# One hold fewer in a scaled copy: the fifth tile loaded whole, the third tile's stores issued right behind that load

## The chip, the core and the metric

The kernel runs on one core of a Trainium2 chip. The core has a vector engine (DVE in the profile), a scalar engine (ACT), a GpSimd engine (POOL), a tensor engine that this kernel doesn't use, and a sync engine (SP) whose sequencer issues DMA transfers. Sixteen DMA engines carry the transfers between the chip's memory (HBM, named "dram" in the profile) and the on-chip memory (SBUF, 128 partitions). The metric is the device time of one execution in microseconds. The kernel before took 239.05 us, the median of three runs (238.97 to 239.15).

## The reference

Each of 16 x 1024 tokens is a row of 512 floats. Each token goes to two experts, and its row is written twice, each time scaled by that expert's weight:

```python
def reference(x, expert_indices, expert_weights):
    batch, seq, hidden = x.shape          # 16, 1024, 512, float32
    k = expert_indices.shape[-1]          # 2
    x_expanded = x[:, :, np.newaxis, :].repeat(k, axis=2)
    weights = expert_weights[..., np.newaxis]
    return (x_expanded * weights).astype(np.float32)
```

The indices' values are not used. The input x has 33.6 MB and the output 67.1 MB, so what is stored is twice what is loaded.

## The kernel before

The 16,384 tokens are 128 per partition. They are cut into five tiles along the tokens of a partition: `groups` = 25, 25, 25, 25 and 28 tokens per partition. A partition's tokens of one tile lie next to each other in the memory, so a transfer has one unbroken row per partition (25 tokens loaded are 51,200 bytes; a stored token is 4,096 bytes, since it is written twice).

Buffers: `x_pair` are two input buffers, used in turn by the tiles (tiles 0, 2, 4 use the first, 1 and 3 the second). `o_ring` is one output buffer of 25 tokens (`TX`), used by every tile, in two parts: tokens 0 to 12 and 13 to 24 (`CUT` = 13). `w_tile` has all weights.

Transfers: `move` issues a DMA from SP and keeps SP's issues in the order of the program. `load(i, e)` loads part e of tile i; `STEPS` says in which parts a tile comes (tile 0 as 9 and 16 tokens, tile 2 as 21 and 4, tile 4 as 24 and 4), and a tile that is not in `STEPS` comes whole. `store(dst, at, to)` writes tokens at to `to` of `o_ring` to the output. `wait(ins, done)` makes the transfer `ins` wait at its issue until the transfer `done` has landed. The framework adds the waits that the data need: a load waits until the tile that used its buffer before has been computed, a store until its half has been computed, and computing a half waits until the ring's half has been stored.

Work on a tile (the loop at the end of the kernel): for each of the two parts of the ring, DVE multiplies the first 8 tokens (9 in tile 0) by their weights in pieces of 4 tokens (`product`, line 97), and ACT the other 4 or 5 tokens, one row at a time (`scalar`, line 120). Then the transfers:

- Tiles 1, 3 and 4 issue each store as soon as its part is computed. Tile 1 also issues the load of tile 3 behind its stores.
- Tiles 0 and 2 are "held": first the load into the buffer that this tile has read (tile 2 or tile 4), in two parts, then the two stores, each made to wait until the first part of that load has landed. Tile 0 issues the weights of the other tiles between.
- Tile 4 has three tokens more than the ring; they are computed and stored at the end.

So SP issues in this order: loads 0, 1, 2 and the weights; stores of 0 (held) and 1; loads 3 and 4; stores of 2 (held), 3 and 4. All of them but the first weights go through one queue of SP (q1 in the profile), on line 66.

Of the kernel before, what the change touches and what calls it, by code (L numbers as in the profile page):

```python
# [1 line left out]

# [4 lines left out]


@with_exitstack
def kernel(  # L10
    ctx: ExitStack,
    tc: tile.TileContext,
    x: bass.AP,
    expert_indices: bass.AP,
    expert_weights: bass.AP,
    out: bass.AP,
):
    nc = tc.nc

    batch, seq, hidden = x.shape  # L20
    k = expert_weights.shape[-1]
    P = nc.NUM_PARTITIONS
    ntok = batch * seq
    assert ntok % P == 0
    A_TOTAL = ntok // P

    f32 = mybir.dt.float32
    row = k * hidden
    CH = 4


    groups = [25, 25, 25, 25, 28]
    TX = 25
    CUT = 13
    STEPS = {0: [9, 16], 2: [21, 4], 4: [24, 4]}
    assert sum(groups) == A_TOTAL

    xf = x.rearrange("b s h -> (b s) h")
    of = out.rearrange("b s k h -> (b s) (k h)")
    wf = expert_weights.rearrange("b s k -> (b s) k")  # L40

    w_pool = ctx.enter_context(tc.tile_pool(name="w_pool", bufs=1))
    x_pool = ctx.enter_context(tc.tile_pool(name="x_pool", bufs=1))
    o_pool = ctx.enter_context(tc.tile_pool(name="o_pool", bufs=1))

    w_tile = w_pool.tile([P, A_TOTAL * k], f32)
    o_ring = o_pool.tile([P, TX * row], f32)
    x_pair = [
        x_pool.tile([P, max(groups[e::2]) * hidden], f32, name=f"x{e}")
        for e in range(2)  # L50
    ]

    def rows(of_all, done, T):
        return of_all[done * P : (done + T) * P, :].rearrange(
            "(p a) n -> p (a n)", a=T
        )

    tiles = []
    done = 0
    for n in groups:  # L60
        tiles.append((done, n))
        done += n


    def move(out, in_):
        return tc.keep_in_program_order(nc.sync.dma_start(out=out, in_=in_))  # L66


    def wait(ins, done):
        tc.add_manual_dep(  # L70
            ins.ins,
            done.ins.name,
            mybir.DependencyInfo(
                mybir.DependencyClass.Sync, mybir.DependencyReason.DATA
            ),
            reason="turn",
        )

    def load(i, e):
        at = sum(STEPS.get(i, groups[i : i + 1])[:e])  # L80
        to = at + STEPS.get(i, groups[i : i + 1])[e]
        part = slice(at * hidden, to * hidden)
        return move(x_pair[i % 2][:, part], rows(xf, *tiles[i])[:, part])

    def weights(g, to):
        at, n = tiles[g]
        w = w_tile[:, at * k : (at + (to - g) * n) * k]
        return (
            w.rearrange("p (g m) -> p g m", g=to - g),
            wf[at * P : (at + (to - g) * n) * P, :].rearrange(  # L90
                "(g p a) n -> p g (a n)", g=to - g, p=P
            ),
        )

    def product(o_tile, t, x_in, c, m):
        o = t * row
        nc.vector.tensor_tensor(  # L97
            out=o_tile[:, o : o + m * row].rearrange(
                "p (t k h) -> p t k h", t=m, k=k
            ),  # L100
            in0=x_in[:, : m * hidden]
            .rearrange("p (t h) -> p t h", t=m)
            .unsqueeze(2)
            .to_broadcast([P, m, k, hidden]),
            in1=w_tile[:, c : c + m * k]
            .rearrange("p (t k) -> p t k", t=m)
            .unsqueeze(3)
            .to_broadcast([P, m, k, hidden]),
            op=mybir.AluOpType.mult,
        )  # L110


    def vector(src, c, at, to):
        for t in range(at, to, CH):
            u = min(t + CH, to)
            product(o_ring, t, src[:, t * hidden : u * hidden], c + t * k, u - t)

    def scalar(src, c, at, to):
        return [
            nc.scalar.mul(  # L120
                out=o_ring[:, e * hidden : (e + 1) * hidden],
                in_=src[:, e // k * hidden : (e // k + 1) * hidden],
                mul=w_tile[:, c + e : c + e + 1],
            )
            for e in range(at * k, to * k)
        ]

    def store(dst, at, to):
        return move(dst[:, at * row : to * row], o_ring[:, at * row : to * row])


    out_w, in_w = weights(0, 1)
    nc.scalar.dma_start(out=out_w, in_=in_w)
    load(0, 0)
    load(0, 1)
    load(1, 0)
    for i, (done, n) in enumerate(tiles):
        src, dst, c = x_pair[i % 2], rows(of, done, n), done * k
        v = 9 if i == 0 else 8
        held = i in (0, 2)  # L140
        for at, to in [(0, CUT), (CUT, TX)]:
            vector(src, c, at, at + v)
            scalar(src, c, at + v, to)
            if not held:
                store(dst, at, to)
        if held:
            if i == 0:
                last = load(2, 0)
                load(2, 1)
                for g in range(1, len(tiles)):  # L150
                    move(*weights(g, g + 1))
            else:
                last = load(4, 0)
                load(4, 1)
            for at, to in [(0, CUT), (CUT, TX)]:
                wait(store(dst, at, to), last)
        elif i == 1:
            load(3, 0)
        if n > TX:
            m = n - TX  # L160
            product(o_ring, 0, src[:, TX * hidden :], c + TX * k, m)
            move(dst[:, TX * row :], o_ring[:, : m * row])

# [1 line left out]
_INS = ['x', 'expert_indices', 'expert_weights']  # L165
_OUTS = [((16, 1024, 2, 512), 'float32')]


# [23 lines left out]
```

## Time and profile before

| | |
|---|---|
| median of 3 runs | 239.05 us |
| the profiled execution's own time | 238.92 us |
| its span, first to last instruction | 237.1 us |
| moved by DMA | 100.80 MB, 425 GB/s over the span |
| DVE busy | 93.1 us (39%) |
| ACT busy | 54.9 us (23%) |
| DMA queue q1 | 98.7% of the 16 engines' span |

The profile is of one execution. Times in it are counted from the start of its span. A line of the timeline or of the chain of waits begins with start and length in microseconds; a group line gives engine, line of the code, operation, what is written and read, and how many. An engine's name with a "q" behind it means its sequencer, which issues transfers and is not counted as busy. For a DMA issue, "us to landing" is the time from its issue to the end of the whole transfer, the time that it spends behind others in the queue included. The DMA share of a stretch is the time of the packets that start in it, over 16 engines and the stretch's length; for a stretch of the length of a few packets it can be far from the busy share, and above 1.

### The profile page before, as it was taken

The numbers are of one execution on the slowest core, as the hardware profiler recorded it, in microseconds if no ns is written. First come the engines' busy times: TensorE is split into PE (matmuls) and PEld (weight loads), VectorE is DVE, ScalarE is ACT, GpSimd is POOL, SyncE is SP. The second block draws the span as 40 slices with busy tenths as digits, with TensorE's granted clock in tenths as the row PEclk, the third lists the DMA queues.
The fourth block names the chain that finished last, engine by engine and source line by source line (L and its number), as shares of the span: only waits on it lengthen the run. The fifth ranks groups of instructions, "written<-read, shape, count | busy, mean of one in ns | idle before, by whom it ended". The sixth has DMA issues, their size and how long they took to land.

```text
span 237.1 us, 217 instructions
## 1 busy us (share of the span) xinstructions
DVE 93.1 (39%) x23; ACT 54.9 (23%) x87; POOL 0.2 (0%) x4
## 2 busy tenths in 40 slices
DVE  0499800000094580954900000039195292861300
ACT  0008800000090520914400000037080270800000
POOL 0000000000000000000000000000000000000000
DMA  7999989899999999999999999999999999999996
GB/s 260 474 445 475 423 370 464 372 486 431 420 398 497 464 431 420 398 398 409 475 478 406 398 453 431 431 409 457 484 431 431 409 398 434 449 449 456 423 398 265
DMA packets 3457, 100.80 MB, mean 425 GB/s; under 512 B 1024, under 2 KB 1024, under 8 KB 1024
## 3 DMA queue, kind: packets, MB, share of 16 engines
q1 hardware_dynamic: 3312, 100.77, 98.7%
q10 hardware_dynamic: 144, 0.03, 0.1%
q14 instruction: 1, 0.01, 0.0%
HBM read 33.69 MB, written 67.11 MB: 425 GB/s over the span
## 4 chain that ended last, share of the span: by engine, by line
DMA 70%; DVE 16%; ACT 4%; issue 3%; SPq 0%; DVEq 0%; ACTq 0%
DMA out_dram<-o_ring 46%; DMA x<-in_x_dram 24%; DVE o_ring L97 16%; ACT o_ring L120 3%; ACT L120 1%; SPq L66 0%; DVEq L97 0%; ACTq L120 0%
## 5 line engine op out<-in xcount | busy, mean ns | idle before, releaser
L97 DVE TENSOR_TENSOR o_ring<-x,w_tile 128x4096 f32<-128x4096 f32 (+2 forms) x23 | 93.1, 4096 | 128.5 <-DMA out_dram<-o_ring 105.6
L120 ACT ACTIVATE o_ring<-x,w_tile 128x512 f32<-128x512 f32 x86 | 53.7, 709 | 134.0 <-DMA out_dram<-o_ring 123.3
L120 ACT ACT_TABLE_LOAD x1 | 1.3, 1283 | 18.6 <-DMA x<-in_x_dram 18.6
L176 POOL MEMSET const-bfloat16-1.0<- 128x1 bf16 x1 | 0.1, 102 | 0.0
L176 POOL MEMSET const-uint8-127<- 128x1 uint8 x1 | 0.1, 102 | 0.0
L176 POOL MEMSET const-float32-0.0<- 128x1 f32 x1 | 0.1, 99 | 0.2 <-issue 0.2
L176 POOL MEMSET const-float32-1.0<- 128x1 f32 x1 | 0.1, 99 | 0.0
## 6 DMA issues: line engine op xcount, KB each, us to landing
out_dram<-o_ring SPq DMA_DIRECT2D x5, 6656.0 KB, 21.3
out_dram<-o_ring SPq DMA_DIRECT2D x5, 6144.0 KB, 21.6
x<-in_x_dram SPq DMA_DIRECT2D x2, 6400.0 KB, 34.1
x<-in_x_dram SPq DMA_DIRECT2D x1, 6144.0 KB, 20.6
x<-in_x_dram SPq DMA_DIRECT2D x1, 5376.0 KB, 18.8
x<-in_x_dram SPq DMA_DIRECT2D x1, 4096.0 KB, 17.4
x<-in_x_dram SPq DMA_DIRECT2D x1, 2304.0 KB, 8.1
x<-in_x_dram SPq DMA_DIRECT2D x2, 1024.0 KB, 21.4
```

What stands on the lines that cost most here:

```text
L97: nc.vector.tensor_tensor(out=o_tile[:, o : o + m * row].rearrange("p (t k h) -> p t k h", t=m, k=k), in0=x_in[:, : m * hidden] .rearrange ...
L120: nc.scalar.mul(out=o_ring[:, e * hidden : (e + 1) * hidden], in_=src[:, e // k * hidden : (e // k + 1) * hidden], mul=w_tile[:, c + e : c ...
L176: nc = _bacc.Bacc("TRN2", target_bir_lowering=False, num_devices=1)
```

## The change

Tile 4 leaves `STEPS`, so it is loaded in one piece of 28 tokens. Tile 2 is no longer held: its two stores are issued right behind the load of tile 4 and wait for nothing but their data. Tile 0 keeps its hold and its order. What the loop did for tiles 1, 3 and 4 stays as it was.

```diff
-    STEPS = {0: [9, 16], 2: [21, 4], 4: [24, 4]}
+    STEPS = {0: [9, 16], 2: [21, 4]}
...
-        held = i in (0, 2)
         for at, to in [(0, CUT), (CUT, TX)]:
             vector(src, c, at, at + v)
             scalar(src, c, at + v, to)
-            if not held:
+            if i in (1, 3, 4):
                 store(dst, at, to)
-        if held:
-            if i == 0:
-                last = load(2, 0)
-                load(2, 1)
-                for g in range(1, len(tiles)):
-                    move(*weights(g, g + 1))
-            else:
-                last = load(4, 0)
-                load(4, 1)
+        if i == 0:
+            last = load(2, 0)
+            load(2, 1)
+            for g in range(1, len(tiles)):
+                move(*weights(g, g + 1))
             for at, to in [(0, CUT), (CUT, TX)]:
                 wait(store(dst, at, to), last)
         elif i == 1:
             load(3, 0)
+        elif i == 2:
+            load(4, 0)
+            store(dst, 0, CUT)
+            store(dst, CUT, TX)
```

## The prediction

> **What bounds the kernel now.** I read the page first, then a table of stretches, then the chain of waits, then the queue's waits, and last single packets of the transfers around the edit.
>
> ```profile
> span 237.1 us, 217 instructions
> ...
> DVE 93.1 (39%) x23; ACT 54.9 (23%) x87; POOL 0.2 (0%) x4
> ...
> DMA  7999989899999999999999999999999999999996
> ...
> q1 hardware_dynamic: 3312, 100.77, 98.7%
> ```
>
> The two computing engines are idle most of the time; the 16 DMA engines are not. The table of stretches (length, busy time of the computing engines, clock, DMA share, GB/s) puts the edges to it:
>
> ```profile
> core 0: us, DVE busy (x) ACT busy (x) POOL busy (x), PEclk, DMA share, GB/s
> 0.00:1.74 1.74, 0.00 (x0) 0.00 (x0) 0.20 (x4) 1.00 0.00 0
> 1.74:235.90 234.16, 93.14 (x23) 54.95 (x87) 0.00 (x0) 1.00 1.00 430
> 235.90:237.10 1.20, 0.00 (x0) 0.00 (x0) 0.00 (x0) 1.00 0.00 0
> ```
>
> From the first packet at 1.74 to the last end at 235.90 the DMA share is 1.00. So the time is 1.74 of lead-in, 234.16 of packets without a gap worth 1%, and 1.20 of drain. Only three things can move it: fewer or shorter packets, a stretch in which the queue would have run dry, or a change in what a packet costs. Whether an engine waits longer or shorter for its data matters only if the queue runs dry through it.
>
> The chain of waits around the edit (start, length, what):
>
> ```profile
> 88.37 21.56 DMA out_dram<-o_ring
> ...
> 118.85 20.61 DMA x<-in_x_dram
> ...
> 139.52 18.14 DMA out_dram<-o_ring
> ...
> 157.85 8.77 DVE o_ring L97 x2
> ...
> 166.68 14.48 DMA out_dram<-o_ring
> ...
> 188.08 8.77 DVE o_ring L97 x2
> ```
>
> Here 88.37 is the second store of the second tile, 118.85 the first part of the fifth tile's load (24 tokens), 139.52 the third tile's first store, which was held until that load had landed (118.85 + 20.61 = 139.46), 157.85 the fourth tile's first half, which needs the ring that this store empties, and 188.08 the fifth tile's. The hold shows as one of SP's three waits for a load:
>
> ```profile
> SPq L66 <- DVE o_ring L97: 168.8, 10, 28.8
> SPq L66 <- DMA x<-in_x_dram: 41.9, 3, 19.8
> ```
>
> The longest, 19.8 us, is the hold that goes. But a wait of the queue's issuer is not a wait of the DMA engines, and the next steps keep the two apart.
>
> **The change part by part.**
>
> *The hold.* If it left the engines without work, the stretch around it would show it. In the same table, with windows cut to the packets (a packet counts with its whole time in the stretch in which it starts, so share times length is the mean packet time of an engine when each of the 16 starts one):
>
> ```profile
> 136.70:142.94 6.24, 0.00 (x0) 0.00 (x0) 0.00 (x0) 1.00 1.01 431
> 142.90:143.60 0.70, 0.00 (x0) 0.00 (x0) 0.00 (x0) 1.00 2.81 1217
> ```
>
> The first row runs from the last packets of the 24-token part, over the 4-token part, through the first packets of the held store. Share 1.01 times 6.24 is 6.30 us of packets in 6.24 us of time: the engines had work throughout. The 4-token part covers the hold (8 packets per engine of 0.31, below, 2.5 us, against about 1.0 from an issue to its first packet, estimated from the first load's issue at 0.73, in the timeline below, and its first packet at 1.74). So taking the hold away wins 0.00. Without that cover the hold would cost about 1 us; the change removes hold and cover together.
>
> *The load in one piece.* Three bands of 16 packets of different row lengths, 12 tokens stored (48 KB), 25 tokens loaded (50 KB), and above at 142.90 13 tokens stored (52 KB):
>
> ```profile
> 105.00:105.70 0.70, 0.00 (x0) 0.00 (x0) 0.00 (x0) 1.00 2.59 1123
> 106.80:107.50 0.70, 0.00 (x0) 0.00 (x0) 0.00 (x0) 1.00 2.75 1123
> 110.70:111.40 0.70, 0.70 (x1) 0.70 (x3) 0.00 (x0) 1.00 2.75 1170
> 112.60:113.30 0.70, 0.70 (x1) 0.70 (x2) 0.00 (x0) 1.00 2.70 1170
> ```
>
> 2.59, 2.70 and 2.81 times 0.70 are 1.813, 1.890 and 1.967 us: 0.077 for each 2 KB more, load or store alike. And inside the 4-token part, 62 packets of 8 KB in 1.2 us:
>
> ```profile
> DMA packets 62, 0.51 MB, mean 423 GB/s; under 512 B 0, under 2 KB 0, under 8 KB 0
> ...
> q1 hardware_dynamic: 62, 0.51, 100.2%
> ```
>
> 1.002 x 16 x 1.2 / 62 = 0.310 us. Each engine serves 8 rows of a tile. Before: 8 x (1.813 + 0.310) = 16.98. After: 8 rows of 56 KB, two steps above 52 KB, 8 x (1.967 + 0.154) = 16.97; no row of 56 KB stands in this trace, so that is an estimate by the slope. One completion mark per engine goes too. Together -0.01 to -0.05; I take -0.03. The bounds of the 56 KB row: if it were cut in two, 8 more packet starts bring back what was saved, 0.00; so -0.05 to 0.
>
> *The stores issued early.* They move from 139.52 to right behind the load, about 119.3 and 119.7 (the load's issue at 118.85, and some 0.4 for each). What is queued then: the rest of the fourth tile's load, the fifth's, and two stores, four transfers. The queue has held more, and keeps order; its rows in the timeline (start, length of all the issues, count):
>
> ```profile
> 0.73 28.38 SPq L66 DMA_DIRECT2D x<-in_x_dram  x5
> ...
> 29.16 1.90 SPq L66 DMA_DIRECT2D w_tile<-in_expert_weights_dram  x4
> ...
> 88.75 1.21 SPq L66 DMA_DIRECT2D x<-in_x_dram  x1
> ...
> 118.85 0.82 SPq L66 DMA_DIRECT2D x<-in_x_dram  x2
> ...
> 139.52 0.82 SPq L66 DMA_DIRECT2D out_dram<-o_ring  x2
> ```
>
> The second row issues weights while three loads are unfinished, at 1.90 / 4 = 0.48 each, so seven transfers are no obstacle. The third, the fourth tile's load, took 1.21 to issue for reasons that I can't see; if a store's issue took as long, it would hide behind the 5 us and more of packets still queued, and SP's next instruction is the wait for the fourth tile's first half, which ends at 166.6. Order, by the issues of 88.5 to 89, of 119.2 to 119.6 and of 139.86 to 141 (KB, us to landing):
>
> ```profile
> x<-in_x_dram SPq DMA_DIRECT2D x1, 6400.0 KB, 36.2
> ...
> x<-in_x_dram SPq DMA_DIRECT2D x1, 1024.0 KB, 22.6
> ...
> out_dram<-o_ring SPq DMA_DIRECT2D x1, 6656.0 KB, 18.1
> out_dram<-o_ring SPq DMA_DIRECT2D x1, 6144.0 KB, 32.4
> ```
>
> The load issued at 88.75 landed at 124.95, that is 15.0 us after the store ahead of it (88.37 + 21.56 = 109.93), and 15.1 is its own 8 x 1.890. It waited its turn. So the early stores will go behind the whole load as they do now, the bytes are in the same order, and the store of 139.52 lands at about 157.6 as before. The computing of the fourth tile then keeps its cover: its store is issued at 166.68, while the second store (139.9 + 32.4) lands at 172.3, so 5.6 us less about 1.0 to a first packet, 4.6 us, are spare. The fifth tile is read at 188.08 at the earliest, the load lands about 142, as its last part does now (119.28 + 22.6 = 141.9): 46 us spare. Cost 0.00. Without the cover every us late would count in full.
>
> *The turn from load to store.* This is the unknown: in the trace every such turn comes after a hold, and none has stores queued long before. Lower bound: the held turn, which has no gap (1.01) and whose second store band (2.81) lies on the slope of the others, 0.00. Upper bound: the other turn, store to load, which is made in queue order with no hold (the second tile's second store to the fourth tile's load). Its last store band and second load band are longer, 2.75 for 2.59 and 2.75 for 2.70, so 0.112 + 0.035 = 0.15 us on the mean of the engines. The slowest engine decides a landing, and the views give no single engine; three times the mean, 0.45, is my estimate of it. I take 0.00, since the direction of the turn is that of the held one, and keep 0 to 0.45.
>
> A rule of the Trainium skill speaks against the change here: DMA: Bandwidth & Descriptors, "Two DMAs through the same engine are not ordered", says that an engine's read and write sides are separate queues and that a later transfer may read while an earlier one still writes. The longer packets at the store-to-load turn agree with it. By it the early stores would read while the load's last packets are written, and the sum would get some of the upper bound.
>
> **Sum.** Span 237.10 - 0.03 + 0.00 + 0.00 + 0.00 = 237.07. The profiled execution took 238.92, so 1.82 lies around its span: 238.89. It was 0.13 below the median of the runs, 239.05; on that scale the forecast is 239.02, rounded 239.0.
>
> **The rivals.**
>
> *A turn that costs.* The unheld turn is stretched as the store-to-load turn is: +0.15 to +0.45, less 0.03: 239.2 to 239.5. For it: the two bands. Against it: a store's reads don't use the memory that the load reads from, while at 107 us a load's reads met a store's writes there. Still inside what counts as no change, for the most part.
>
> *Slower: stores in waiting slow the load.* With stores queued from 119.3, the fifth tile's load packets run beside reads for the stores, each band stretched like the last store band at 106.80: 0.112 x 8 bands, +0.90, 239.9. It decides from 0.064 us a band (0.48 + 0.03 over 8). Against it: the fourth tile's load was queued from 88.75 on, and the store band at 105.00 ran undisturbed at 2.59; only the last band ahead of the turn was touched.
>
> *Faster: the hold had a price after all.* If landing, wait and issue left the engines dry for what lies between issue and first packet, about 1.0, the time would be 238.0. Against it stands the share of 1.01 in the row of 136.70; for it only that this row is made of packet records and not of a measured idle time. The Trainium skill puts about 2 us of fixed cost on a transfer, most of it the receipt (same page, "Anatomy of one DMA — SWDGE (gpsimd) path"); by it an uncovered hold would give back 2 us, 237.0, but no idle of that size is in this trace.
>
> **How the numbers follow.** The forecast has a chance of 0.60, the costly turn 0.17, the slowed load 0.16, the dry hold 0.07. About 0.2%, 0.48 us, is what a measurement of this kernel can tell from no change: forecast and costly turn lie within it, 0.77; slower 0.16; faster 0.07. The range leaves out the last two but for a part: from 238.6, the forecast less the spread of the runs and some of the third rival, to 239.7, the upper bound of the turn with the 0.13 by which single runs differ.
>
> **What would show it.** Right: SP's waits for a load fall from three to two and from 41.9 to about 22; SP instead waits some 46 us for the fourth tile's first half; the stores show about 38 and 52 us from issue to landing for 18.1 and 32.4, and still land near 157.6 and 172.3; the load of 7168 KB lands near 142; the DMA share between first and last packet stays 1.00; the fourth tile's first half begins near 157.8. Wrong: load bands between 124 and 141 of more than 2.12 us an engine, a first store band above 1.97, or a landing of the first store before the load's, which would break the order. The forecast as a whole falls if the span moves by more than 0.5 us.

## The result, and the profile after

The changed kernel takes 239.49 us, the median of 16 runs (239.28 to 239.68), the kernel before in the same comparison 238.97 us (238.75 to 239.22). The ratio is 1.0023, 95% interval 1.0016 to 1.0029: 0.52 us slower, which is small, and clear of the noise. No change had been forecast, so the direction was missed.

The page of the changed kernel, the lines that were shown of before:

```profile
span 237.8 us, 212 instructions
...
DVE 93.2 (39%) x23; ACT 55.0 (23%) x87; POOL 0.2 (0%) x4
...
DMA  7999989899999999999999799999999999999996
...
q1 hardware_dynamic: 3168, 100.77, 98.7%
```

The same bytes, the same share of the queue, but 0.7 us more span. A slice of 7 in the DMA row is no gap: a packet counts where it starts, and few start there. In the table of stretches (length, busy times, clock, DMA share, GB/s) the share from first to last packet is still 1.00:

```profile
1.74:236.60 234.86, 93.15 (x23) 54.95 (x87) 0.00 (x0) 1.00 1.00 429
```

So nothing ran dry; packets took longer. The chain of waits of the changed kernel shows where the delay comes in (start, length, what):

```profile
88.46 21.50 DMA out_dram<-o_ring
...
118.87 0.34 SPq L66
...
119.26 39.09 DMA out_dram<-o_ring
...
158.43 8.77 DVE o_ring L97 x2
...
167.26 14.46 DMA out_dram<-o_ring
...
188.63 8.77 DVE o_ring L97 x2
```

The store ahead of the turn landed at 109.96, 0.03 later than before. The third tile's first store landed at 119.26 + 39.09 = 158.35, where it had been 157.66: 0.69 later. Behind it 0.58 us is left at the fourth tile's first half (158.43 for 157.85) and 0.55 at the fifth tile's (188.63 for 188.08). The issues of 118.8 to 119.9 (KB, us to landing) say the same of the load: it landed at 118.87 + 23.8 = 142.7 instead of 141.9.

```profile
x<-in_x_dram SPq DMA_DIRECT2D x1, 7168.0 KB, 23.8
out_dram<-o_ring SPq DMA_DIRECT2D x1, 6656.0 KB, 39.1
...
out_dram<-o_ring SPq DMA_DIRECT2D x1, 6144.0 KB, 53.1
```

Single bands of 16 packets, in windows cut to them (share times length is the mean packet time):

```profile
106.80:107.55 0.75, 0.00 (x0) 0.00 (x0) 0.00 (x0) 1.00 2.55 1049
...
136.70:137.42 0.72, 0.00 (x0) 0.00 (x0) 0.00 (x0) 1.00 2.94 1274
138.80:139.55 0.75, 0.00 (x0) 0.00 (x0) 0.00 (x0) 1.00 3.62 1223
...
143.40:144.27 0.87, 0.00 (x0) 0.00 (x0) 0.00 (x0) 1.00 2.26 979
```

The seventh band of the load takes 2.94 x 0.72 = 2.12 us, its eighth and last 3.62 x 0.75 = 2.72. The stores behind it are undisturbed (2.26 x 0.87 = 1.97). The whole loss is in the last load packet of each engine, 0.60 us on the mean. The turn from store to load at 106.8 is stretched as before (2.55 x 0.75 = 1.91 for 1.81).

### The profile page after: what moved, and what is told of

The parts are those of the page before. It is cut to its first block, busy times and chain, and to the rows that moved or that the text cites. A ratio compares the mean times of both kernels' runs of the same rounds, so it can differ in the third digit from the quotient of the medians.

```text
span 237.8 us, 212 instructions
## 1 busy us (share of the span) xinstructions
DVE 93.2 (39%) x23; ACT 55.0 (23%) x87; POOL 0.2 (0%) x4
## 4 chain that ended last, share of the span: by engine, by line
DMA 70%; DVE 16%; ACT 4%; issue 3%; SPq 0%; DVEq 0%; ACTq 0%
DMA out_dram<-o_ring 54%; DVE o_ring L97 16%; DMA x<-in_x_dram 15%; ACT o_ring L120 3%; ACT L120 1%; SPq L66 0%; DVEq L97 0%; ACTq L120 0%
## 6 DMA issues: line engine op xcount, KB each, us to landing
x<-in_x_dram SPq DMA_DIRECT2D x1, 7168.0 KB, 23.8
```

## The experiments

The kernel before was timed beside each group: 238.83 us for the first four, 239.00 for the next four, 238.99 for the last three. "First turn" is from the third tile's load to the first tile's stores at 46 to 50 us, "second turn" the changed one at 139 to 142. The time given first is the median of a kernel's executions. The stretches are read from one profiled execution, which lay up to 0.4 us above or below the median; where that matters, it is said.

### The hold, or the size of the last packets

The change did two things at once, it took the hold away and it made the last load packets long. This run takes only the hold away.

```diff
-    STEPS = {0: [9, 16], 2: [21, 4]}
+    STEPS = {0: [9, 16], 2: [21, 4], 4: [24, 4]}
...
             load(4, 0)
+            load(4, 1)
             store(dst, 0, CUT)
```

> The changed kernel, but the fifth tile's load comes in 24 and 4 tokens again, still with no hold: stores queued early, last load packets of 8 KB. In the changed kernel the last band of load packets (56 KB rows) took 2.71 us an engine where the seven before it took 2.12. Theory 1, the hold is what spares the turn (a store that is queued early stretches whatever load packets run last): +0.6 us stays, spread over the last 8 KB packets, time 239.5. Theory 2, the size of the last load packets decides (only a long last row is caught with its store behind it): the 8 KB packets stay at 0.31, at most a few tenths more in all, time about 239.0 as before. No theory expects under 238.8.

239.84 us, ratio 1.0042 (1.0029 to 1.0054). In the trace, first 1.2 us in the middle of the 8 KB packets, then a window from the last band of the 24-token part to the second band of the store, which was 6.24 us long in the kernel before:

```profile
DMA packets 54, 0.44 MB, mean 369 GB/s; under 512 B 0, under 2 KB 0, under 8 KB 0
...
q1 hardware_dynamic: 54, 0.44, 114.9%
```

```profile
136.64:143.39 6.75, 0.00 (x0) 0.00 (x0) 0.00 (x0) 1.00 1.01 398
```

The small packets take 1.149 x 16 x 1.2 / 54 = 0.41 us for 0.31, and the stretch is 0.5 us longer. Theory 1 holds, theory 2 falls: the stretch doesn't need long rows at the end. This run differs from the kernel before in the hold alone. The profiled execution took 239.49 us, 0.66 above the kernel before, which fits the stretch; it was the fastest of the five, and the median is 1.0 above. Where the other 0.35 us come from isn't known.

The counterpart, stores issued late behind long rows, was tried with a load cut by partitions:

```diff
+    CUTP = 112
...
-            load(4, 0)
-            store(dst, 0, CUT)
-            store(dst, CUT, TX)
+            n4 = groups[4] * hidden
+            last = move(x_pair[0][:CUTP, :n4], rows(xf, *tiles[4])[:CUTP, :n4])
+            move(x_pair[0][CUTP:, :n4], rows(xf, *tiles[4])[CUTP:, :n4])
+            for at, to in [(0, CUT), (CUT, TX)]:
+                wait(store(dst, at, to), last)
```

> The fifth tile's load is cut by partitions instead of tokens: 112 partitions, then the last 16, rows of 56 KB in both; the stores are held until the 112 have landed, so they are issued about 2 us ahead of the turn, and the last packet of each engine is a long one. Theory 1 (the hold spares the turn): last band at about 2.12, time 239.0. Theory 2 (the size of the last packet decides): last band about 2.7, time 239.5.

256.41 us, ratio 1.0737 (1.0722 to 1.0751), which no theory had: both parts of this load are slow. Two bands of the 112 partitions take 3.72 x 1.10 = 4.09 us and 2.60 x 1.15 = 2.99 for the same 56 KB that take 2.12 in a transfer of 128 partitions, and the packets of the last 16 partitions 3.30 x 2.20 = 7.26. Why is not known.

```profile
131.65:132.75 1.10, 0.00 (x0) 0.00 (x0) 0.00 (x0) 1.00 3.72 834
135.70:136.85 1.15, 0.00 (x0) 0.00 (x0) 0.00 (x0) 1.00 2.60 798
...
149.80:152.00 2.20, 0.00 (x0) 0.00 (x0) 0.00 (x0) 1.00 3.30 417
```

So this run says nothing of the turn.

### What the hold costs without its cover

```diff
-            load(4, 0)
-            store(dst, 0, CUT)
-            store(dst, CUT, TX)
+            last = load(4, 0)
+            for at, to in [(0, CUT), (CUT, TX)]:
+                wait(store(dst, at, to), last)
```

> The fifth tile loaded whole and the stores held until all of it has landed: no cover and nothing queued. Both theories expect last load packets of 2.12 and then an idle gap: landing, wait, issue to first packet, 1.0 to 2.0 us, time 240.0 to 241.0. It prices the hold without its cover, which the prediction put at about 1 us.

240.82 us, ratio 1.0085 (1.0071 to 1.0099). The last load band and the stretch from it to the first store packet:

```profile
138.79:139.21 0.42, 0.00 (x0) 0.00 (x0) 0.00 (x0) 1.00 5.04 2185
...
138.79:142.67 3.88, 0.00 (x0) 0.00 (x0) 0.00 (x0) 1.00 0.55 236
```

The band is not stretched (5.04 x 0.42 = 2.12). A share of 0.55 of the 3.88 us is 2.13 us of packets. That leaves 1.75 us, a little of which is the end of the band before (the packets start spread over some 0.4 us): about 1.7 us idle. So a hold without cover costs more than the turn without a hold (+2.0 against +0.5 us), and the covered hold of the kernel before is the cheapest of the three.

### Every turn, or this one

```diff
-    STEPS = {0: [9, 16], 2: [21, 4]}
+    STEPS = {0: [9, 16]}
...
-            last = load(2, 0)
-            load(2, 1)
             for g in range(1, len(tiles)):
                 move(*weights(g, g + 1))
-            for at, to in [(0, CUT), (CUT, TX)]:
-                wait(store(dst, at, to), last)
+            load(2, 0)
+            store(dst, 0, CUT)
+            store(dst, CUT, TX)
```

> As the changed kernel, and the first held turn is made the same way: the third tile loaded whole (25 tokens) with the first tile's stores right behind it, no hold; the weights of the later tiles are issued ahead of that load. If the stretch belongs to every load-to-store turn with long rows queued up to a store, a second band of about 2.5 (1.89 + 0.6) appears ahead of the first store and the time is about 240.0 (239.5 + 0.5). If the stretch belongs to the fifth tile's load alone (its 56 KB rows, or its place), the first turn stays at 1.89 and the time is 239.5.

239.58 us, ratio 1.0034 (1.0021 to 1.0048), and neither reading is right:

```profile
44.45:45.00 0.55, 0.00 (x0) 0.00 (x0) 0.00 (x0) 1.00 3.44 1489
46.34:46.89 0.55, 0.00 (x0) 0.00 (x0) 0.00 (x0) 1.00 4.98 1489
107.60:108.40 0.80, 0.00 (x0) 0.00 (x0) 0.00 (x0) 1.00 2.27 983
139.35:140.10 0.75, 0.00 (x0) 0.00 (x0) 0.00 (x0) 1.00 2.86 1223
```

The first turn pays 2.74 - 1.89 = 0.85 us. The last store band ahead of the turn from store to load, stretched in the kernels so far, is now at 2.27 x 0.80 = 1.82, and the second turn is nearly free, 2.145 for 2.12. Two theories could say so: the price is paid once (A), or it depends on how many transfers went through the queue before (B). The next two runs are meant to tell them apart.

```diff
-            for g in range(1, len(tiles)):
-                move(*weights(g, g + 1))
+            move(*weights(1, 4))
+            move(*weights(4, 5))
```

> The changed kernel with the weights of tiles 1 to 3 in one transfer instead of three, so two transfers fewer have gone through the queue when the turn comes; nothing else differs. Both-turns-unheld showed a stretch of 0.85 us at the first turn and 0.03 at the second, which leaves two theories. Theory A (paid once: the first turn that comes with its stores already queued pays, later ones are free): the fifth tile's last band stays at about 2.7, time 239.5. Theory B (place in the queue: whether a turn is stretched depends on how many transfers went before): the band falls to 2.12 or changes clearly, time 239.0.

239.53 us, ratio 1.0025 (1.0015 to 1.0035). The last two load bands:

```profile
136.65:137.15 0.50, 0.00 (x0) 0.00 (x0) 0.00 (x0) 1.00 4.24 1835
138.75:139.25 0.50, 0.00 (x0) 0.00 (x0) 0.00 (x0) 1.00 5.91 1835
```

The stretch stays, 2.96 for 2.12, larger than in the changed kernel, though this is one execution each (here 239.81 us, 0.28 above the median). The other way, one transfer more in the kernel with both turns unheld:

```diff
-    STEPS = {0: [9, 16]}
+    STEPS = {0: [9, 16], 2: [21, 4]}
...
             load(2, 0)
+            load(2, 1)
```

> Both turns unheld, but the third tile's load in 21 and 4 tokens: one transfer more, so that the second turn has the place in the queue that it has in the changed kernel. Theory A (paid once): about 0.85 us of stretch over the packets ahead of the first store, about 0 ahead of the store at 142, time 239.6. Theory B (place): 0.6 ahead of the store at 142 as in the changed kernel, time 240.1 or, where the first turn becomes free, 239.5.

239.96 us, ratio 1.0037 (1.0025 to 1.0050). The 8 KB packets ahead of the first turn, in 1.2 us from 47.0, and the last load band ahead of the second turn:

```profile
DMA packets 45, 0.37 MB, mean 307 GB/s; under 512 B 0, under 2 KB 0, under 8 KB 0
...
q1 hardware_dynamic: 45, 0.37, 106.2%
```

```profile
139.20:140.45 1.25, 0.00 (x0) 0.00 (x0) 0.00 (x0) 1.00 1.77 734
```

0.45 us a packet for 0.31 at the first turn, 2.21 for 2.12 at the second. B expected 0.6 us there, or a free first turn, so on the mean of the engines B falls and A holds. The time doesn't go with A as well: 239.96 is nearer to B's 240.1 than to A's 239.6. A window that holds one packet alone, the one that starts last in that band, shows more, and so do the second tile's second store and the third tile's first in the chain of waits:

```profile
140.40:140.45 0.05, 0.00 (x0) 0.00 (x0) 0.00 (x0) 1.00 3.33 1147
```

```profile
89.62 21.28 DMA out_dram<-o_ring
...
120.22 38.95 DMA out_dram<-o_ring
```

This packet takes 3.33 x 16 x 0.05 = 2.66 us, 0.55 more than undisturbed, and the landing moved by about as much. From landing to landing, 110.90 to 159.17, it is 48.27 us, where the kernel before had 47.73 (109.93 to 157.66) and the changed kernel 48.39. So in this execution (240.37 us, the slowest of its five) the second turn was almost free for most engines, and still cost about 0.5 us in time. A is the better of the two theories, and is not the whole account.

### Paid once in a run, or once after each hold

The turn from store to load gets a hold, first in the kernel before:

```diff
-            if not held:
+            if i == 1 and at == CUT:
+                back = store(dst, at, to - 2)
+                store(dst, to - 2, to)
+            elif not held:
                 store(dst, at, to)
...
-            load(3, 0)
+            wait(load(3, 0), back)
```

> The kernel before, with a hold at the turn from store to load too: the second tile's second store in 10 and 2 tokens, and the fourth tile's load held until the 10 have landed (the last 2 cover it for 2.5 us). If early queued transfers stretch this turn as well, the 0.11 us on the last store band and the 0.04 on the second load band go, less about 0.05 for the extra packets: time 0.1 us below the kernel before, 238.85. If that stretch has another cause it stays, and the time is that of the kernel before or 0.05 above.

239.49 us, ratio 1.0025 (1.0015 to 1.0034): dearer, not cheaper. The stretch of 108.58 to 109.4 has 16 store packets of 8 KB, 16 completion marks and the first 16 load packets; a window shows the second load band:

```profile
DMA packets 48, 0.95 MB, mean 1159 GB/s; under 512 B 16, under 2 KB 16, under 8 KB 16
...
q1 hardware_dynamic: 48, 0.95, 324.1%
```

```profile
110.91:111.92 1.01, 1.01 (x2) 1.01 (x3) 0.00 (x0) 1.00 1.97 811
```

3.241 x 0.82 = 2.66 us an engine, less 0.31 and about 0.01 for the store packet and the mark, leaves 2.34 for a load packet of 1.89; the second takes 1.99. So 0.45 + 0.10 where the unheld turn paid 0.15, and now in the load's first packets instead of the store's last. A hold is not good at every turn: this one is cheaper with its load in the queue.

The same hold between two unheld turns:

```diff
-            if i in (1, 3, 4):
+            if i == 1 and at == CUT:
+                back = store(dst, at, to - 2)
+                store(dst, to - 2, to)
+            elif i in (1, 3, 4):
                 store(dst, at, to)
...
-            load(3, 0)
+            wait(load(3, 0), back)
```

> Both turns from load to store unheld, and the turn from store to load between them held (10 and 2 tokens, as in the earlier run with that hold). If the price is paid once in a run, the second turn stays free: about 0.85 us at the first turn, about 0 ahead of the store at 142; time 239.6 plus what the hold between costs. If it is paid whenever the queue has been let run short before, the hold between brings it back: about 0.6 us again on the last load band ahead of the second turn, time above 240.

242.60 us, ratio 1.0151 (1.0137 to 1.0165). The last load band of the first turn, and the last two of the second:

```profile
46.36:46.96 0.60, 0.00 (x0) 0.00 (x0) 0.00 (x0) 1.00 4.27 1365
...
137.68:139.48 1.80, 0.00 (x0) 0.00 (x0) 0.00 (x0) 1.00 1.18 510
139.78:141.68 1.90, 0.00 (x0) 0.00 (x0) 0.00 (x0) 1.00 1.64 483
```

2.56 at the first turn, 0.67 above 1.89. At the second 1.64 x 1.90 = 3.12 for 2.12, a full us. So the second turn was free, or nearly so on the mean, only in the runs with no hold between. The whole time is longer than these stretches explain; the band of 139.78 is spread over 1.9 us where it was 0.75 in the run without the hold, so the hold has driven the engines apart as well. What share of the second turn's price is due to that is open.

### How early is too early

Three runs keep the kernel before and its hold, and move the hold's end with the tokens of the last part:

```diff
-    STEPS = {0: [9, 16], 2: [21, 4], 4: [24, 4]}
+    STEPS = {0: [9, 16], 2: [21, 4], 4: [14, 14]}
```

> The kernel before, held, with the fifth tile in 14 and 14 tokens instead of 24 and 4: the hold ends some 8 us ahead of the turn instead of 2.5. If a hold as such spares the turn, no stretch and 239.0. If what counts is only that the stores aren't in the queue yet when the load's last 2 us of packets run, the hold ends too early and the 28 KB packets ahead of the first store are stretched by some 0.6 us in all, time 239.5.

239.31 us, ratio 1.0015 (1.0006 to 1.0024). One undisturbed band of 28 KB packets and the last two:

```profile
134.65:135.25 0.60, 0.00 (x0) 0.00 (x0) 0.00 (x0) 1.00 1.78 765
138.94:139.50 0.56, 0.00 (x0) 0.00 (x0) 0.00 (x0) 1.00 2.33 819
140.26:140.91 0.65, 0.00 (x0) 0.00 (x0) 0.00 (x0) 1.00 2.25 706
```

1.07, then 1.30 and 1.46: 0.63 us in all, in spite of a hold. (This execution took 239.59 us; the median is 0.31 above the kernel before, about half of that stretch.) The other two have 20 and 8, and 22 and 6 tokens (the same line edited).

> The kernel before with the fifth tile in 20 and 8 tokens: the hold ends about 5 us ahead of the turn, and the stores reach the queue some 3.5 us ahead of it (issue to first packet 1.46 in the kernel before). Where the stretch needs the store queued when the last 2 to 2.5 us of load packets run, it pays in full, about 0.6 us in the last load bands, time 239.4. Where half a tile ahead was needed, there is no stretch, time 239.0.

> The kernel before with the fifth tile in 22 and 6 tokens: the stores reach the queue some 2.2 us ahead of the turn, between the 1.0 of the kernel before (no stretch) and the 3.5 of 8 tokens. If the window is 2 to 2.5 us, part of the stretch, 0.2 to 0.5 us, time 239.2; if any queued store pays alike, 0.6.

With 8 tokens 239.35 us, ratio 1.0019 (1.0010 to 1.0028); the last three bands of 16 KB packets:

```profile
139.10:139.56 0.46, 0.00 (x0) 0.00 (x0) 0.00 (x0) 1.00 1.33 570
139.70:140.18 0.48, 0.00 (x0) 0.00 (x0) 0.00 (x0) 1.00 1.91 546
140.60:141.23 0.63, 0.00 (x0) 0.00 (x0) 0.00 (x0) 1.00 1.23 416
```

0.61, 0.92, 0.77: 0.47 us. With 6 tokens 239.08 us, ratio 1.0003 (0.9994 to 1.0012); the 12 KB packets from 139.4 to 140.4:

```profile
DMA packets 35, 0.43 MB, mean 430 GB/s; under 512 B 0, under 2 KB 0, under 8 KB 0
...
q1 hardware_dynamic: 35, 0.43, 103.0%
```

1.03 x 16 / 35 = 0.47 us for some 0.46 by the slope. The last bands lie behind that window; a window over all, from the last band of the 22-token part (44 KB rows) to the second store band, is 7.38 us long, for 1.66 + 8 x 0.46 + 1.97 = 7.31 by the slope:

```profile
135.58:142.96 7.38, 0.00 (x0) 0.00 (x0) 0.00 (x0) 1.00 1.01 426
```

That is next to nothing, where 0.2 to 0.5 in all had been expected. When the stores were issued, by the timelines of the runs with 8 and with 6 tokens:

```profile
136.99 0.82 SPq L66 DMA_DIRECT2D out_dram<-o_ring  x2
```

```profile
138.32 0.82 SPq L66 DMA_DIRECT2D out_dram<-o_ring  x2
```

The turn is at about 141. Stores issued 1.5 us ahead of it (139.52, the kernel before) or 2.7 us (138.32) leave it free; 4 us ahead (136.99) most of the price is there. Whether microseconds count or what is still ahead in the queue is not told apart: by the lengths of the packets, a store had about 5 packets of 8 KB or 6 of 12 KB ahead of it on an engine in the two free runs, and about 6.5 of 16 KB or 7 of 28 KB (issued at 133.63) in the two that paid.

## Why the prediction was wrong

**The turn from load to store** is the step that failed. The prediction put it at 0.00 with a bound of 0.45, "since the direction of the turn is that of the held one". It measured 0.60 on the mean of the engines, and 0.69 at the landing. Two of the signs that the prediction had named for being wrong came: a load band of more than 2.12 us, and a span more than 0.5 us longer. The direction was the wrong likeness. What sets the two turns apart is how early the stores were issued: 1.5 to 2.7 us ahead was free, 4 us or more was not. The run without the hold, with all else as before, and the three runs that move the hold's end show that. The upper bound came from the store-to-load turn, and that is a different thing: holding it makes it dearer.

**The rival "a turn that costs"**, at a chance of 0.17, was right in kind and too small: it allowed 0.12 to 0.42 us, and 0.52 was measured. That 239.49 lies in its 239.2 to 239.5 is luck, since the kernel before was 0.08 us faster in this comparison than in the one that the rival was counted from. Its size was taken from two bands of another turn, and the argument against it, that a store's reads and a load don't share a memory, was only an argument; the trace had no unheld load-to-store turn to support it. Beside those two bands, what spoke for it was the Trainium skill's sentence on separate read and write sides of an engine (DMA: Bandwidth & Descriptors, "Two DMAs through the same engine are not ordered"). The measurements agree with it as far as they go: the stretch lies on the last load packets and not on the stores. That the store's reads are what holds them up is not shown.

**What hides the hold** was right: no idle at the covered hold, so nothing to win. Its price without cover was put at about 1 us, and is about 1.7 us of idle and 2.0 in the time; only the way to the first packet had been counted, not the landing and the wait. The rival "a price after all" got no support.

**The 56 KB row** was right: 2.12 us by the slope, 2.12 measured, so the whole load wins nothing that can be measured.

**Order, depth of the queue and cover of the computing** were right. The store landed behind the load, the issues took hardly longer (0.92 us for the two stores, 0.82 before), and SP's waits turned as forecast:

```profile
SPq L66 <- DVE o_ring L97: 189.4, 10, 47.0
SPq L66 <- DMA x<-in_x_dram: 22.2, 2, 15.3
```

19.7 us less wait at SP bought nothing, since SP was never the bound.

**The rival "slowed load"** is wrong in its place: only the last band is stretched, not all eight. That its time, 239.9, was not far off is chance.

**The border of no change.** The prediction took 0.48 us as what can be told from no change, and gave 0.77 to what lies within it. The measured 0.52 lies just outside.

## What to carry over

Where a DMA queue is the bound, look at each turn between loads and stores band by band, and not only for idle time: a queue that is busy 100% can still lose time in stretched packets. At a turn from loads to stores, a store issued 1.5 to 2.7 us ahead was free here, one issued 4 us ahead or earlier stretched the last load packets by 0.5 to 0.85 us the first time (0.3 to 1.0 us in the median times); a hold with a small transfer behind it (here 4 to 6 tokens of 28) gets the free case, and a hold without that cover costs more than it saves. Take each hold by itself: the one from store to load cost 0.5 us.

## What was not expected of the hardware

The price is paid mostly once: with both turns unheld the first cost 0.85 us, the second 0.03, and the turn from store to load between them became free too; in the run with the third tile's load in two parts the second cost 0.09 on the mean, but 0.55 on the engine that came last. In the one run with a hold in between the price came back. It looks like a state of the engines that is built up at the first turn and lost when the queue runs short, but no view shows that state, and it stays open.

A load of 112 partitions instead of 128 took 3.0 to 4.1 us for a row of 56 KB instead of 2.12, and one of 16 partitions 7.3 (256.41 us in all).
